# A mean over rows on one core: rewritten so that a partition owns 128 neighbouring rows, with loops, aligned buffers and one store

## The chip, the cores and the metric

The kernel runs on one core of a Trainium2 chip. The metric is the device time of one execution in microseconds (us); the median of the timed runs stands for a kernel. The core's engines are TensorE (PE, matrix products), VectorE (DVE), ScalarE (ACT), GpSimd (POOL) and SyncE (SP, which here only issues transfers). Each has its own program; they meet at semaphores. Sixteen DMA engines move data between the device memory (DRAM) and the on-chip memory (SBUF), which has 128 partitions; a tensor there has rows in partitions and columns along each of them. PSUM is a small memory that TensorE writes.

## The reference

```python
def setup_inputs():
    return {"x": np.random.randn(64, 256, 8192).astype(np.float32)}

def reference(x):
    return np.mean(x, axis=2)
```

So 64 x 256 = 16,384 rows of 8192 numbers (32 KiB) each become one number: 512 MiB are read, 64 KiB are written.

## The kernel before, in words

The input is seen as 16,384 rows. The kernel works in tiles of 256 rows (8 MiB): a partition of a tile gets two neighbouring rows, 64 KiB in one piece, into one of three buffers. `NB` = 63 tiles are done so; the last 256 rows are handled apart, as two tiles of 128 rows, `T0` and `T1`.

Which two rows a partition gets is set by the view `pairs`: partition 4m+w holds rows 64w+2m and 64w+2m+1 of the tile. So partitions 0, 4, 8 ... hold neighbouring pieces of 64 KiB, and partitions 0 to 3 hold pieces that lie 64 rows (2 MiB) apart.

The programs are unrolled: every tile has its own instructions on every engine.

- SP issues the load of tile g into buffer g mod 3 (line 106), after waiting until VectorE (line 104 or 105) and ScalarE have summed tile g-3. Then come `T0` in one load (line 109) and `T1` in seven loads of falling width (line 111): 4096, 2048, 1024, 512, 256, 128 and 128 columns, the last of them into the tensor `fin`. Then the stores: 63 KiB of results (line 115) and two rows of 128 results (line 118).
- VectorE sums the first row of each pair (line 129), ScalarE the second one, by a copy onto itself with a running total (line 153). In the last tile they share the one row of a partition by halves (lines 133, 139, 143 and 153); VectorE adds the partial sums (lines 136 and 147).
- The sums lie one per partition, and the result must lie along a row to be stored in long pieces: TensorE transposes them by an identity matrix that GpSimd builds (lines 87, 89, 184, 186, 189), and ScalarE copies them from PSUM, scaled by 1/8192 (line 157).

All loads and stores go through SP's one queue, in the order of issue. Semaphores count tiles done by VectorE (`dve_sem`) and ScalarE (`act_sem`), and landings for each buffer (`in_sems`).

The buffers are the first tensors of the kernel. The program's own placement puts them at byte 16,512 of each partition, 65,536 bytes apart; 16,512 is 64.5 times 256.

Of the kernel before, what the change touches and what calls it, by code (L numbers as in the profile page):

```python
# [4 lines left out]

F32 = mybir.dt.float32
ADD = mybir.AluOpType.add
X = mybir.AxisListType.X
COPY = mybir.ActivationFunctionType.Copy


def bass_global_avg_pool_1d_kernel(
    nc: bass.Bass,
    x: bass.AP,
    out: bass.AP,
):
    P = 128
    B, C, L = x.shape
    rows = B * C
    assert rows % (2 * P) == 0 and L % 64 == 0  # L20
    inv = 1.0 / float(L)

    NB = rows // (2 * P) - 1
    NBUF = 3
    assert NB >= NBUF

    flat = x.rearrange("b c l -> (b c) l")
    W = 4  # L30
    M = P // W
    pairs = flat.rearrange("(g w m j) l -> g m w (j l)", w=W, m=M, j=2)
    tiles = flat.rearrange("(t p) l -> t p l", p=P)
    T0, T1 = 2 * NB, 2 * NB + 1
    out_flat = out.rearrange("b c -> (b c)")
    out_pairs = out_flat.rearrange("(g q) -> g q", q=2 * P)
    out_tiles = out_flat.rearrange("(t p) -> t p", p=P)

    ch = [L // 2, L // 4, L // 8, L // 16, L // 32, L // 64, L // 64]
    assert sum(ch) == L
    NCH = len(ch)
    NS = 4
    offs = [sum(ch[:c]) for c in range(NCH)]
    NPART = 2 * NS + 2

    with ExitStack() as ctx:
        sb = lambda n, s: ctx.enter_context(nc.sbuf_tensor(n, s, F32))
        ps = lambda n, s: ctx.enter_context(nc.psum_tensor(n, s, F32))  # L50
        sem = lambda n: ctx.enter_context(nc.semaphore(n))
        bufs = [sb(f"buf{i}", [P, 2 * L]) for i in range(NBUF)]
        in_sems = [sem(f"in_sem{i}") for i in range(NBUF)]
        res = [sb(f"res{j}", [P, NB]) for j in range(2)]

        fin = sb("fin", [P, ch[-1] + NPART])
        half = sb("half", [P, 2])
        last = [sb(f"last{j}", [P, 1]) for j in range(2)]
        ident = sb("ident", [P, P])
        outsb = sb("outsb", [NB, 2 * P])  # L60
        row = [sb(f"row{j}", [1, P]) for j in range(2)]
        psum = [ps(f"psum{j}", [NB, P]) for j in range(2)]
        psum_row = [ps(f"psum_row{j}", [1, P]) for j in range(2)]
        dve_sem = sem("dve_sem")
        act_sem = sem("act_sem")
        ident_sem = sem("ident_sem")
        pe_sem = sem("pe_sem")
        cp_sem = sem("cp_sem")
        tile_sem = sem("tile_sem")
        out_sems = [sem(f"out_sem{i}") for i in range(3)]  # L70
        ch_sems = [sem(f"ch_sem{i}") for i in range(NCH)]
        pd_sem = sem("pd_sem")
        pa_sem = sem("pa_sem")

        tail = bufs[NB % NBUF]
        H = L // 2
        tile0 = tail[:, 0:L]
        part = lambda i: fin[:, ch[-1] + i : ch[-1] + i + 1]

        def chunk(c):  # L80
            if c == NCH - 1:
                return fin[:, 0 : ch[c]]
            return tail[:, L + offs[c] : L + offs[c] + ch[c]]


        eng = nc.gpsimd
        eng.memset(ident[:], 0.0).then_inc(ident_sem, 1)  # L87
        eng.wait_ge(ident_sem, 1)
        eng.affine_select(  # L89
            out=ident[:],  # L90
            in_=ident[:],
            compare_op=mybir.AluOpType.not_equal,
            fill=1.0,
            base=0,
            pattern=[[-1, P]],
            channel_multiplier=1,
        ).then_inc(ident_sem, 1)


        eng = nc.sync  # L100
        for g in range(NB):
            b = g % NBUF
            if g >= NBUF:
                eng.wait_ge(dve_sem, g - NBUF + 1)
                eng.wait_ge(act_sem, g - NBUF + 1)
            eng.dma_start(bufs[b][:], pairs[g]).then_inc(in_sems[b], 16)
        eng.wait_ge(dve_sem, NB - NBUF + 1)
        eng.wait_ge(act_sem, NB - NBUF + 1)
        eng.dma_start(tile0, tiles[T0]).then_inc(tile_sem, 16)  # L109
        for c in range(NCH):  # L110
            eng.dma_start(  # L111
                chunk(c), tiles[T1][:, offs[c] : offs[c] + ch[c]]
            ).then_inc(ch_sems[c], 16)
        eng.wait_ge(cp_sem, 2)
        eng.dma_start(out_pairs[0:NB, :], outsb[:, :]).then_inc(out_sems[0], 16)
        for j in range(2):
            eng.wait_ge(cp_sem, 3 + j)
            eng.dma_start(out_tiles[T0 + j : T0 + j + 1, :], row[j][:, :]).then_inc(
                out_sems[1 + j], 16
            )  # L120
        for s in out_sems:
            eng.wait_ge(s, 16)


        eng = nc.vector
        for g in range(NB):
            b = g % NBUF
            eng.wait_ge(in_sems[b], 16 * (g // NBUF + 1))
            eng.tensor_reduce(  # L129
                res[0][:, g : g + 1], bufs[b][:, 0:L], X, ADD  # L130
            ).then_inc(dve_sem, 1)
        eng.wait_ge(tile_sem, 16)
        eng.tensor_reduce(half[:, 0:1], tile0[:, 0:H], X, ADD).then_inc(dve_sem, 1)  # L133
        eng.wait_ge(act_sem, NB + 1)
        eng.wait_ge(dve_sem, NB + 1)
        eng.tensor_reduce(last[0][:], half[:], X, ADD).then_inc(dve_sem, 1)  # L136
        for c in range(NS):
            eng.wait_ge(ch_sems[c], 16)
            eng.tensor_reduce(part(c), chunk(c)[:, 0 : ch[c] // 2], X, ADD).then_inc(  # L139
                pd_sem, 1  # L140
            )
        eng.wait_ge(ch_sems[NCH - 2], 16)
        eng.tensor_reduce(part(NS), chunk(NCH - 2), X, ADD).then_inc(pd_sem, 1)  # L143
        eng.wait_ge(pa_sem, NS + 1)
        eng.wait_ge(ch_sems[NCH - 1], 16)
        eng.wait_ge(pd_sem, NS + 1)
        eng.tensor_reduce(last[1][:], fin[:], X, ADD).then_inc(dve_sem, 1)  # L147


        eng = nc.scalar  # L150

        def summed(ap, to, done):
            eng.activation(ap, ap, COPY, accum_out=to).then_inc(done, 1)  # L153

        def from_psum(n, dst, src):
            eng.wait_ge(pe_sem, n)
            eng.activation(dst, src, COPY, scale=inv).then_inc(cp_sem, 1)  # L157

        for g in range(NB):
            b = g % NBUF  # L160
            eng.wait_ge(in_sems[b], 16 * (g // NBUF + 1))
            summed(bufs[b][:, L : 2 * L], res[1][:, g : g + 1], act_sem)
        for j in range(2):
            from_psum(
                j + 1,
                outsb[:, :].rearrange("g (w m j) -> g j m w", w=W, m=M, j=2)[:, j],
                psum[j][:, :].rearrange("g (m w) -> g m w", m=M, w=W),
            )
        eng.wait_ge(tile_sem, 16)
        summed(tile0[:, H:L], half[:, 1:2], act_sem)  # L170
        for c in range(NS):
            eng.wait_ge(ch_sems[c], 16)
            summed(chunk(c)[:, ch[c] // 2 :], part(NS + 1 + c), pa_sem)
            if c == 0:
                from_psum(3, row[0][:, :], psum_row[0][:, :])
        eng.wait_ge(ch_sems[NS], 16)
        summed(chunk(NS), part(NPART - 1), pa_sem)
        from_psum(4, row[1][:, :], psum_row[1][:, :])


        eng = nc.tensor
        eng.wait_ge(ident_sem, 2)
        eng.wait_ge(dve_sem, NB)
        eng.transpose(psum[0][:, :], res[0][:, :], ident[:, :]).then_inc(pe_sem, 1)  # L184
        eng.wait_ge(act_sem, NB)
        eng.transpose(psum[1][:, :], res[1][:, :], ident[:, :]).then_inc(pe_sem, 1)  # L186
        for j in range(2):
            eng.wait_ge(dve_sem, NB + 2 + j)
            eng.transpose(psum_row[j][:, :], last[j][:, :], ident[:, :]).then_inc(  # L189
                pe_sem, 1  # L190
            )


# [26 lines left out]
```

## Time and profile before

| what | value |
|---|---|
| timed runs | 1247.22, 1247.23, 1247.58 us; median 1247.23 |
| span of the profiled execution, first to last instruction | 1246.1 us |
| around the span, to the median | 1.2 us |
| DMA | 536.97 MB, 10,303 packets, mean 431 GB/s |
| VectorE busy | 556.9 us (45%) |
| ScalarE busy | 459.2 us (37%) |
| TensorE and GpSimd busy | 1.4 and 0.7 us |

The profiled execution's own time is its span and what lies around it; the timed runs carry no profile of their own, so the 1.2 us is the span set against their median. A line of a group reads: line of the kernel, engine, operation, result<-source, shapes and number of instructions | busy time in us, mean ns of one | idle time of the engine ahead of them, and what ended it. The chain of waits follows the work back from the last instruction and is shown in order of time: start, length in us, and what it was; "issue" is time in which nothing recorded was waited for. The rows of digits show the busy share of 40 equal slices of the span in tenths.

### The profile page before, as it was taken

The page shows a single profiled execution, that of the slowest core. Times are in us where ns is not written, and L with a number is a line of the kernel's source. Part 1 is how long each engine was busy: PE and PEld are TensorE (multiplying, and loading weights), DVE is VectorE, ACT ScalarE, POOL GpSimd, SP SyncE. Part 2 cuts the span into 40 slices and gives each one's busy share as a digit, 9 for nine tenths or more (in the row PEclk, how much of TensorE's full clock was granted, in tenths as well). Part 3 has the DMA queues.
Part 4 walks back from the last instruction along what each step waited for, and adds up shares of the span by engine and source line. Part 5 has one row for each costly group of instructions (what it writes and reads, how often), then busy time and mean ns, then how long its engine had stood idle before and what let it go on. Part 6 is the DMA issues. An engine that isn't in the chain of part 4 may idle for free.

```text
span 1246.1 us, 383 instructions
## 1 busy us (share of the span) xinstructions
PE 1.4 (0%) x4; PEld 0.4 (0%) x4; DVE 556.9 (45%) x71; ACT 459.2 (37%) x143; POOL 0.7 (0%) x6
## 2 busy tenths in 40 slices
PE   0000000000000000000000000000000000000000
PEld 0000000000000000000000000000000000000000
DVE  2354453543534435345354453544535435344355
ACT  2243342442423424334243342433424324234245
POOL 0000000000000000000000000000000000000000
DMA  9999999999999999999999999999999999999998
GB/s 404 438 438 438 435 421 425 435 438 438 438 438 435 425 421 435 438 438 438 438 435 429 419 434 438 438 438 438 432 431 423 433 435 438 435 438 433 433 425 362
DMA packets 10303, 536.97 MB, mean 431 GB/s; under 512 B 1147, under 2 KB 1596, under 8 KB 1852
## 3 DMA queue, kind: packets, MB, share of 16 engines
q1 hardware_dynamic: 10300, 536.94, 99.7%
q14 instruction: 3, 0.02, 0.0%
HBM read 536.87 MB, written 0.07 MB: 431 GB/s over the span
## 4 chain that ended last, share of the span: by engine, by line
DMA 85%; DVE 15%; ACT 0%; SPq 0%; issue 0%; PE 0%
DMA buf<-in_x_dram 85%; DVE res L129 15%; ACT buf L153 0%; SPq L111 0%; PE psum_row L189 0%; SPq L109 0%; DVE last L147 0%; ACT row L157 0%
## 5 line engine op out<-in xcount | busy, mean ns | idle before, releaser
L129 DVE TENSOR_REDUCE res<-buf 128x1 f32<-128x8192 f32 x63 | 547.2, 8686 | 685.4 <-DMA buf<-in_x_dram 685.4
L153 ACT ACTIVATE buf<-buf 128x8192 f32<-128x8192 f32 (+3 forms) x69 | 450.9, 6535 | 782.0 <-DMA buf<-in_x_dram 782.0
L153 ACT ACTIVATION_READ_ACCUMULATOR buf<-buf 128x1 f32 x69 | 12.9, 187 | 0.0
L133 DVE TENSOR_REDUCE half<-buf 128x1 f32<-128x4096 f32 x1 | 4.4, 4420 | 1.0 <-DMA buf<-in_x_dram 1.0
L139 DVE TENSOR_REDUCE fin<-buf 128x1 f32<-128x2048 f32 (+3 forms) x4 | 4.5, 1153 | 0.5 <-DMA buf<-in_x_dram 0.4
L184 PE MATMUL psum<-ident,res 128*63 128x128 f32 x1 | 0.4, 444 | 1232.8 <-DVE res L129 1232.8
L153 ACT ACT_TABLE_LOAD x1 | 1.3, 1283 | 0.7 <-PEq L205 0.7
L157 ACT ACTIVATE outsb<-psum 63x128 f32<-63x128 f32 x2 | 0.6, 389 | 2.2 <-PE psum L184 2.2
L157 ACT ACTIVATE row<-psum_row 1x128 f32<-1x128 f32 x2 | 0.5, 258 | 0.8 <-PE psum_row L189 0.8
L189 PE MATMUL psum_row<-ident,last 128*1 128x128 f32 x2 | 0.7, 372 | 10.5 <-DVE last L147 5.5
L184 PEld LDWEIGHTS psum<-ident,res 128*63 128x63 f32 x1 | 0.2, 179 | 1232.7 <-issue 1232.7
L186 PE MATMUL psum<-ident,res 128*63 128x128 f32 x1 | 0.4, 421 | 0.0
L147 DVE TENSOR_REDUCE last<-fin 128x1 f32<-128x138 f32 x1 | 0.3, 297 | 0.1
L143 DVE TENSOR_REDUCE fin<-buf 128x1 f32<-128x128 f32 x1 | 0.3, 286 | 0.1
L89 POOL TENSOR_SCALAR_AFFINE_SELECT ident<-ident 128x128 f32<-128x128 f32 x1 | 0.3, 292 | 0.2 <-POOL ident L87 0.2
L186 PEld LDWEIGHTS psum<-ident,res 128*63 128x63 f32 x1 | 0.2, 230 | 0.0
L87 POOL MEMSET ident<- 128x128 f32 x1 | 0.2, 204 | 0.3 <-POOLq L205 0.3
L136 DVE TENSOR_REDUCE last<-half 128x1 f32<-128x2 f32 x1 | 0.2, 155 | 0.1
L189 PEld LDWEIGHTS psum_row<-ident,last 128*1 128x1 f32 x2 | 0.2, 79 | 11.2 <-DVE last L147 5.8
L205 POOL MEMSET const-bfloat16-1.0<- 128x1 bf16 x1 | 0.1, 101 | 0.0
L205 POOL MEMSET const-uint8-127<- 128x1 uint8 x1 | 0.1, 101 | 0.0
L205 POOL MEMSET const-float32-0.0<- 128x1 f32 x1 | 0.1, 98 | 0.2 <-issue 0.2
(1 smaller groups left out, 0.1 us busy)
## 6 DMA issues: line engine op xcount, KB each, us to landing
buf<-in_x_dram SPq DMA_DIRECT2D x1, 4096.0 KB, 39.7
buf<-in_x_dram SPq DMA_DIRECT2D x1, 2048.0 KB, 44.1
buf<-in_x_dram SPq DMA_DIRECT2D x1, 1024.0 KB, 46.1
buf<-in_x_dram SPq DMA_DIRECT2D x63, 49.3
buf<-in_x_dram SPq DMA_DIRECT2D x1, 512.0 KB, 47.0
buf<-in_x_dram SPq DMA_DIRECT2D x1, 256.0 KB, 47.1
buf<-in_x_dram SPq DMA_DIRECT2D x1, 128.0 KB, 47.0
buf<-in_x_dram SPq DMA_DIRECT2D x1, 64.0 KB, 46.7
```

Source lines behind the costliest of these rows:

```text
L89: eng.affine_select(out=ident[:], in_=ident[:], compare_op=mybir.AluOpType.not_equal, fill=1.0, base=0, pattern=[[-1, P]], channel_multipl ...
L129: eng.tensor_reduce(res[0][:, g : g + 1], bufs[b][:, 0:L], X, ADD).then_inc(dve_sem, 1)
L133: eng.tensor_reduce(half[:, 0:1], tile0[:, 0:H], X, ADD).then_inc(dve_sem, 1)
L139: eng.tensor_reduce(part(c), chunk(c)[:, 0 : ch[c] // 2], X, ADD).then_inc(pd_sem, 1)
L143: eng.tensor_reduce(part(NS), chunk(NCH - 2), X, ADD).then_inc(pd_sem, 1)
L147: eng.tensor_reduce(last[1][:], fin[:], X, ADD).then_inc(dve_sem, 1)
L153: eng.activation(ap, ap, COPY, accum_out=to).then_inc(done, 1)
L157: eng.activation(dst, src, COPY, scale=inv).then_inc(cp_sem, 1)
L184: eng.transpose(psum[0][:, :], res[0][:, :], ident[:, :]).then_inc(pe_sem, 1)
L186: eng.transpose(psum[1][:, :], res[1][:, :], ident[:, :]).then_inc(pe_sem, 1)
L189: eng.transpose(psum_row[j][:, :], last[j][:, :], ident[:, :]).then_inc(pe_sem, 1)
L205: nc = _bacc.Bacc("TRN2", target_bir_lowering=False, num_devices=1)
```

## The change

A partition now owns 128 neighbouring rows (4 MiB of the input): partition p has rows 128p to 128p+127. Tile i takes rows 2i and 2i+1 of every partition, again 64 KiB in one piece for each, and the pieces of a tile lie 4 MiB apart. The two last rows of each partition take the place of `T0` and `T1`; the last one comes in six loads (4096, 2048, 1024, 512, 256 and 256 columns) instead of seven.

SP, VectorE and ScalarE run loops over three tiles each (21 rounds) instead of unrolled programs; addresses of loads, results and waits are computed from the loop's counter. One semaphore per buffer (`free_sems`) is raised by both VectorE and ScalarE and replaces the two counts. ScalarE's table load stands inside its loop, ahead of the first sum.

The results of a partition are now neighbours in the output, so nothing is transposed: TensorE, PSUM and the identity are gone. ScalarE scales as it sums, into every second column of `outsb`; VectorE scales its 63 sums in one instruction, and adds and scales the partial sums of the last two rows with `total`. One store of 128 partitions with 512 bytes each stands at the end.

The small tensors are allocated ahead of the buffers, padded to multiples of 256 bytes; `pad0` and `pad1` hold nothing. The buffers begin at byte 24,576 of each partition, 96 times 256.

```diff
@@ -21,174 +22,145 @@
     inv = 1.0 / float(L)
+    R = rows // P
+    NBUF = 3
+    NLOOP = (R // 2 - 1) // NBUF
+    assert NLOOP * NBUF == R // 2 - 1 and NLOOP >= 2
...
-    W = 4
-    M = P // W
-    pairs = flat.rearrange("(g w m j) l -> g m w (j l)", w=W, m=M, j=2)
-    tiles = flat.rearrange("(t p) l -> t p l", p=P)
...
-    out_pairs = out_flat.rearrange("(g q) -> g q", q=2 * P)
...
+    own = x.rearrange("b c l -> (b c) l").rearrange("(p r) l -> p (r l)", p=P)
+    out_own = out.rearrange("b c -> (b c)").rearrange("(p r) -> p r", p=P)
-    ch = [L // 2, L // 4, L // 8, L // 16, L // 32, L // 64, L // 64]
+    ch = [L // 2, L // 4, L // 8, L // 16, L // 32, L // 32]
     assert sum(ch) == L
     NCH = len(ch)
-    NS = 4
+    NS = NCH - 2
     offs = [sum(ch[:c]) for c in range(NCH)]
-    NPART = 2 * NS + 2
+    NPART = 2 * NS + 1
     with ExitStack() as ctx:
         sb = lambda n, s: ctx.enter_context(nc.sbuf_tensor(n, s, F32))
...
         sem = lambda n: ctx.enter_context(nc.semaphore(n))
+        sb("pad0", [P, 32])
+        fin = sb("fin", [P, 320])
+        scaled = sb("scaled", [P, 320])
+        half = sb("half", [P, 64])
+        scaled_half = sb("scaled_half", [P, 64])
+        res = sb("res", [P, R])
+        outsb = sb("outsb", [P, R])
+        sb("pad1", [P, 960])
         bufs = [sb(f"buf{i}", [P, 2 * L]) for i in range(NBUF)]
         in_sems = [sem(f"in_sem{i}") for i in range(NBUF)]
-        res = [sb(f"res{j}", [P, NB]) for j in range(2)]
+        free_sems = [sem(f"free_sem{i}") for i in range(NBUF)]
+        row_sem = sem("row_sem")
+        ch_sems = [sem(f"ch_sem{i}") for i in range(NCH)]
+        act_sem = sem("act_sem")
+        dve_sem = sem("dve_sem")
+        out_sem = sem("out_sem")
...
-        psum_row = [ps(f"psum_row{j}", [1, P]) for j in range(2)]
...
+        tail = bufs[0]
         H = L // 2
...
         def chunk(c):
             if c == NCH - 1:
                 return fin[:, 0 : ch[c]]
             return tail[:, L + offs[c] : L + offs[c] + ch[c]]
...
+        part = lambda i: fin[:, ch[-1] + i : ch[-1] + i + 1]
         eng = nc.sync
-        for g in range(NB):
...
-            eng.dma_start(bufs[b][:], pairs[g]).then_inc(in_sems[b], 16)
...
-        eng.dma_start(tile0, tiles[T0]).then_inc(tile_sem, 16)
+        for b in range(NBUF):
+            eng.dma_start(bufs[b][:], own[:, 2 * b * L : 2 * (b + 1) * L]).then_inc(
+                in_sems[b], 16
+            )
+        with eng.Fori(1, NLOOP) as i:
+            for b in range(NBUF):
+                eng.wait_ge(free_sems[b], i * 2)
+                eng.dma_start(
+                    bufs[b][:], own[:, bass.ds((i * NBUF + b) * (2 * L), 2 * L)]
+                ).then_inc(in_sems[b], 16)
+        eng.wait_ge(free_sems[0], 2 * NLOOP)
+        eng.dma_start(tail[:, 0:L], own[:, (R - 2) * L : (R - 1) * L]).then_inc(
+            row_sem, 16
+        )
         for c in range(NCH):
-            eng.dma_start(
...
-        eng.dma_start(out_pairs[0:NB, :], outsb[:, :]).then_inc(out_sems[0], 16)
...
-            eng.dma_start(out_tiles[T0 + j : T0 + j + 1, :], row[j][:, :]).then_inc(
...
+            a = (R - 1) * L + offs[c]
+            eng.dma_start(chunk(c), own[:, a : a + ch[c]]).then_inc(ch_sems[c], 16)
+        D_SCALE, D_HALF, D_ROW = 1, 2, 3
+        D_PART = D_ROW + NS + 1
+        D_LAST = D_PART + 1
+        A_HALF = 1
+        A_PART = A_HALF + NS
+        eng.wait_ge(dve_sem, D_LAST)
+        eng.dma_start(out_own, outsb[:]).then_inc(out_sem, 16)
+        eng.wait_ge(out_sem, 16)
         eng = nc.vector
-        for g in range(NB):
...
-            eng.tensor_reduce(
...
+        with eng.Fori(0, NLOOP) as i:
+            for b in range(NBUF):
+                eng.wait_ge(in_sems[b], i * 16 + 16)
+                eng.tensor_reduce(
+                    res[:, bass.ds(i * NBUF + b, 1)], bufs[b][:, 0:L], X, ADD
+                ).then_inc(free_sems[b], 1)
+        def total(to, junk, ap, after):
+            eng.wait_ge(dve_sem, after)
+            eng.tensor_scalar(
+                junk, ap, inv, None, MULT, ADD, accum_out=to
             ).then_inc(dve_sem, 1)
...
-        eng.tensor_reduce(half[:, 0:1], tile0[:, 0:H], X, ADD).then_inc(dve_sem, 1)
...
-        eng.tensor_reduce(last[0][:], half[:], X, ADD).then_inc(dve_sem, 1)
...
+        for b in range(NBUF):
+            eng.wait_ge(free_sems[b], 2 * NLOOP)
+        n = R // 2 - 1
+        eng.tensor_scalar(
+            outsb[:, 0 : R - 2].rearrange("p (n j) -> p j n", j=2)[:, 0],
+            res[:, 0:n],
+            inv,
+            None,
+            MULT,
+        ).then_inc(dve_sem, 1)
+        eng.wait_ge(row_sem, 16)
+        eng.tensor_reduce(half[:, 0:1], tail[:, 0:H], X, ADD).then_inc(dve_sem, 1)
+        eng.wait_ge(act_sem, A_HALF)
+        total(outsb[:, R - 2 : R - 1], scaled_half[:, 0:2], half[:, 0:2], D_HALF)
+        for c in range(NS + 1):
             eng.wait_ge(ch_sems[c], 16)
-            eng.tensor_reduce(part(c), chunk(c)[:, 0 : ch[c] // 2], X, ADD).then_inc(
...
-        eng.tensor_reduce(part(NS), chunk(NCH - 2), X, ADD).then_inc(pd_sem, 1)
...
+            share = chunk(c)[:, 0 : ch[c] // 2] if c < NS else chunk(c)
+            eng.tensor_reduce(part(c), share, X, ADD).then_inc(dve_sem, 1)
+        eng.wait_ge(act_sem, A_PART)
         eng.wait_ge(ch_sems[NCH - 1], 16)
...
-        eng.tensor_reduce(last[1][:], fin[:], X, ADD).then_inc(dve_sem, 1)
+        w = ch[-1] + NPART
+        total(outsb[:, R - 1 : R], scaled[:, 0:w], fin[:, 0:w], D_PART)
         eng = nc.scalar
+        with eng.Fori(0, NLOOP) as i:
+            for b in range(NBUF):
+                eng.wait_ge(in_sems[b], i * 16 + 16)
+                ap = bufs[b][:, L : 2 * L]
+                eng.activation(
+                    ap,
+                    ap,
+                    COPY,
+                    scale=inv,
+                    accum_out=outsb[:, bass.ds((i * NBUF + b) * 2 + 1, 1)],
+                ).then_inc(free_sems[b], 1)
-        def summed(ap, to, done):
...
+        def summed(ap, to):
+            eng.activation(ap, ap, COPY, accum_out=to).then_inc(act_sem, 1)
-        def from_psum(n, dst, src):
...
-        for g in range(NB):
...
-            summed(bufs[b][:, L : 2 * L], res[1][:, g : g + 1], act_sem)
...
-        summed(tile0[:, H:L], half[:, 1:2], act_sem)
+        eng.wait_ge(row_sem, 16)
+        summed(tail[:, H:L], half[:, 1:2])
         for c in range(NS):
             eng.wait_ge(ch_sems[c], 16)
-            summed(chunk(c)[:, ch[c] // 2 :], part(NS + 1 + c), pa_sem)
...
-        summed(chunk(NS), part(NPART - 1), pa_sem)
...
-        eng.transpose(psum[0][:, :], res[0][:, :], ident[:, :]).then_inc(pe_sem, 1)
...
-        eng.transpose(psum[1][:, :], res[1][:, :], ident[:, :]).then_inc(pe_sem, 1)
...
-            eng.transpose(psum_row[j][:, :], last[j][:, :], ident[:, :]).then_inc(
...
+            summed(chunk(c)[:, ch[c] // 2 :], part(NS + 1 + c))
 # ---- launch: one core; inputs and outputs as the reference has them ----
```

## The prediction

> **What bounds the kernel now.** I read the page first, for who is busy. The DMA rows come first, then the two compute rows:
>
> ```profile
> DVE  2354453543534435345354453544535435344355
> ACT  2243342442423424334243342433424324234245
> DMA  9999999999999999999999999999999999999998
> ...
> q1 hardware_dynamic: 10300, 536.94, 99.7%
> ...
> L129 DVE TENSOR_REDUCE res<-buf 128x1 f32<-128x8192 f32 x63 | 547.2, 8686 | 685.4 <-DMA buf<-in_x_dram 685.4
> L153 ACT ACTIVATE buf<-buf 128x8192 f32<-128x8192 f32 (+3 forms) x69 | 450.9, 6535 | 782.0 <-DMA buf<-in_x_dram 782.0
> ```
>
> One queue keeps the 16 DMA engines busy for 99.7% of the span; VectorE and ScalarE are half idle, and all of that idle time before their big sums ends with a landing. The chain of waits, in order of time, gives the beat:
>
> ```profile
> 23.34 8.70 DVE res L129
> 32.04 0.02 issue
> 32.05 49.32 DMA buf<-in_x_dram
> 81.37 0.02 issue
> 81.40 8.70 DVE res L129
> ...
> 1242.31 0.02 issue
> 1242.33 1.54 ACT buf L153 x6
> 1243.87 0.03 issue
> 1243.90 0.31 DVE last L147
> 1244.21 0.04 issue
> 1244.26 0.39 PE psum_row L189
> 1244.64 0.02 issue
> 1244.66 0.27 ACT row L157
> ```
>
> From 23.34 to 81.40 three tiles of 8 MiB land: 58.06 us, 19.35 each, 433 GB/s. VectorE needs 8.7 of each 19.35. So 63 tiles make 1219 us of the 1246.1, and only two things can move the time: what one packet costs a DMA engine, and the pieces at both ends (the first tile lands at 23.3, some 4 us more than a beat; from the last landings to the end some 3.8 us).
>
> The trace also keeps one record per DMA packet. A big load is 128 packets of 65,536 bytes, eight on each engine, back to back. In the first tiles an engine starts one every 2414 ns; later every 2414 to 2429 ns, 2419 on average (19.35/8).
>
> **The change part by part.** The profiled execution spans 1246.06 us; the median of the timed runs is 1247.23, so 1.17 us lie around the span. I change the sum against the span and add the 1.17 back.
>
> *Buffers at multiples of 256 bytes.* Before, the buffers begin at byte 16,512 of a partition (128 past such a multiple), after at 24,576. The 512-byte packets of the last loads start 23.5 ns apart, the big ones 2414. The difference, 2390.5 ns over 65,024 bytes, is 36.8 ps a byte; 512 bytes are then 18.8 ns, and 4.7 ns of every packet, large or small, are not bytes. After, an engine has 63x8 + 7x8 = 560 packets. If the placement causes all of it, 2.63 us go; if none, 0. Against: the 4-byte semaphore packet, which has nothing to do with the buffers, also holds its engine some 6 ns. For: all loads, whatever their size, show the same extra, and all begin 128 bytes off. I take 2.63 and keep 0 for a rival. The Trainium skill's page "DMA: Bandwidth & Descriptors", section "How a descriptor splits into AXI transactions", says that a transfer starting off a 256-byte boundary pays for the bytes below its start, in beats of 32 bytes; four beats for 128 bytes would be the 4.7 ns, and the sum by it is the one I take.
>
> *What the packets lose later.* 19.353 less 8x2.414 and 0.006 is 0.035 us a tile, 2.2 us over 63. The trace doesn't show the cause; the pattern repeats from tile to tile, so other addresses may end it (-2.2), leave it (0) or worsen it (the rival on pitch). No row is nearer to either end of a gain; I take half, -1.1.
>
> *A partition owns 128 neighbouring rows.* A tile's 128 blocks of 64 KiB lay in four runs, neighbours 64 KiB apart; now each lies 4 MiB from the next. Sizes, counts and order of issue stay. The nearest row is the last tiles' loads, with rows 32 KiB apart: their 32,768-byte packets take 1213 to 1224 ns, the same time per byte. So a pitch changed by half cost nothing, and I take 0; but that row is far away, and the upper end stands among the rivals.
>
> *Loops.* Each engine's program becomes a loop of three tiles: registers, a branch, waits against register values. SP has issued three tiles ahead, so a late issue is covered by two queued tiles, 38.7 us. VectorE has 10.7 us idle per tile, ScalarE 12.2. ScalarE's table load now stands inside the loop: 21 times 1.28 us, one per three tiles, within that idle time. Were the cover gone, because a load took less than about 9 us a tile, these would count; it can't. Cost 0. The two semaphores per buffer become one that both engines raise: the same later one decides.
>
> *The last sums.* Before, ScalarE's six sums end at 1243.87, then VectorE, the transpose and ScalarE's copy run to 1244.93. After, ScalarE has one sum less (done near 1243.5), and VectorE runs on from 1242.33: 512 columns 0.69, 256 columns 0.42, the whole fifth piece of 256 another 0.42, so 1243.9, and then a scaling sum over 265 columns. Sums of 138 and 256 columns took 0.297 and 0.419; 265 are 0.43, and up to 0.62 if the running total has to be read out as ScalarE's does (0.187). The result is there at 1244.36 to 1244.55: 0.38 to 0.57 earlier, I take 0.45. TensorE's transposes, the copies from PSUM and GpSimd's identity go; all but the last ones lay beside loads and are worth 0. One load less (eight 4.7 ns packets' overhead and a semaphore) is 0.05.
>
> *One store.* Before, the last thing was one row of 512 bytes: 1244.93 to the end at 1246.06, 1.13 us, while the 63 KiB store lay hidden. Now all 64 KiB, 128 packets, go at the end, behind the last sum, with SP waiting for nothing else. Low end: as before plus eight packets on an engine, +0.2. High end: the first load, also 128 packets into an idle queue, was issued at 0.73; ten engines began between 2.17 and 2.30, the last one at 3.64, 2.9 after issue; with 0.2 and the 0.37 from the last packet to the end that is 3.48, +2.35. I go by the ten: 1.57+0.2+0.37, +1.0.
>
> Sum: -2.63 -1.1 -0.45 -0.05 +1.0 = -3.2. Span 1242.8, time 1244.0 us, 0.26% less. A measurement of this kernel tells about 0.2% (2.5 us) from no change.
>
> **The rivals.**
>
> 1. *The placement brings nothing.* Per-packet cost is the engine's own. For it: the semaphore packet. Against: the equal extra on all loads. Then +0 to -2.2, -0.5, +0.2 to +2.35: 1245.0 to 1249.1, most likely 1246.8, no change.
> 2. *The pitch slows the loads a little.* If every packet took what the slow ones take now, 2429 ns for 2419, 504 of them add 5 us, and without the 1.1: 1250. It decides once a packet lengthens by over 6.3 ns (3.2 us over 504). For it: packets differ by up to 15 ns today, so the loads do feel something.
> 3. *The pitch slows the loads greatly.* Sixteen blocks read at once, at addresses equal in their low 22 bits, could ask for the same part of the memory at the same time, every time, and nothing in the program would spread them again. The only slow packets of this trace are the first sixteen, all engines starting together: 2.42 to 3.64 us, median 3.30. At 3.30 throughout: 504x3.30 = 1663, the last two rows 19.4x1.365 = 27, some 9 at both ends: about 1700 us. Then the ends don't matter. For it: no load of this trace has a pitch above 64 KiB within a run, so none shows that it is harmless. Against: those first packets may be start-up alone, the second ones already take 2418, and the halved pitch changes nothing. The same page, section "Latency and other measured facts", reports copies within the memory at half the rate when rows lie 4 MiB apart and full rate with 4 KiB more, and guesses at aliasing. By its ratio, 103 to 214, this kernel would take some 2,550 us (an estimate from that page); no run here shows such a pitch.
>
> **How the numbers follow.** Forecast 0.37 (its own range 1242.0, all ends good, to 1244.7); rival 1 0.16, of it 0.02 slower by over 0.2%; rival 2 0.13; rival 3 0.34. Faster is the forecast, 0.37; within 0.2% the rest of rival 1, 0.14; slower 0.02+0.13+0.34 = 0.49. The forecast is the likeliest single case, though the slower ones together outweigh it. The range goes from 1242 to 1705: half of rival 3 (0.17) may lie above, 0.02 below.
>
> **What would show it.** Held rate: three tiles in 58.06 us or less in the chain, GB/s at 433 or above, VectorE's idle time before its sum still 10.6 us a tile. Placement: packets starting 2409 to 2410 ns apart, three tiles in 57.95. Store: some 2.1 us from its issue to the end; last sum at 0.43 to 0.62. Wrong: longer waits of VectorE and ScalarE for landings, GB/s below 430 in all slices alike (rivals 2 and 3), or a beat unchanged to the nanosecond (rival 1).

## The result, and the profile after

| kernel | timed runs, us | ratio to before (95% interval) |
|---|---|---|
| before | 1247.22 to 1247.58, median 1247.3 | 1 |
| changed | 1635.86, 1656.65, 1706.20, 1719.98; median 1681.43 | 1.3198 (1.3114 to 1.3283) |

The changed kernel is slower by about a third, and its own time varies by 5% from run to run; the ratio goes by its two faster runs (mean 1646.3 us), and the profile is of one of the two slower ones (span 1704.9 us), a difference on which nothing below rests.

The page of the changed kernel, cut to the lines that answer to those shown of before:

```profile
span 1704.9 us, 759 instructions
...
DVE  2242423233242424233242323424324324433344
...
DMA  8999999999999999999999999999999999999997
GB/s 271 309 304 295 308 315 308 301 295 317 301 309 303 300 298 312 320 306 311 304 320 323 303 315 303 323 323 321 318 329 331 335 331 329 354 360 369 360 383 181
...
q1 hardware_dynamic: 10224, 536.94, 98.5%
...
L109 DVE TENSOR_REDUCE res<-buf 128x8192 f32 x63 | 547.2, 8686 | 1128.9 <-DMA buf<-in_x_dram 1128.9
```

The DMA engines are as busy as before (98.5% against 99.7%) and move the same bytes, but at some 300 GB/s in place of 433, rising to 383 towards the end. VectorE's sums take the same 8686 ns each; its idle time ahead of them grew from 685 to 1129 us, 444 us, and all of it ends with a landing (the arrival of a load's data). The span grew by 459. So "busy" says nothing here about speed: a packet holds its engine longer.

The trace's packet records say the same (65,536-byte packets, 8064 of them; "by time" are means over the first, the eleventh and the last twentieth of them, in order of start):

| kernel | least, ns | median | mean | by time |
|---|---|---|---|---|
| before | 2415 | 2422 | 2423 | 2448 / 2421 / 2421 |
| changed | 2415 | 3334 | 3268 | 3395 / 3331 / 2685 |

504 packets on each engine by 3268 ns are 1647 us. The least packet is as short as before: some packets still pass at the old rate.

### The profile page after: what moved, and what is told of

Read it like the earlier page. It is cut to its first block, busy times and chain, and to the rows that moved or that the text cites. A ratio compares the mean times of both kernels' runs of the same rounds, so it can differ in the third digit from the quotient of the medians.

```text
span 1704.9 us, 759 instructions
## 1 busy us (share of the span) xinstructions
DVE 557.4 (33%) x74; ACT 483.7 (28%) x157; POOL 0.2 (0%) x4
## 3 DMA queue, kind: packets, MB, share of 16 engines
q1 hardware_dynamic: 10224, 536.94, 98.5%
## 4 chain that ended last, share of the span: by engine, by line
another core or an unknown queue 75%; DVE 23%; DMA 2%; issue 0%; DVEq 0%
DVE res L109 22%; DMA buf<-in_x_dram 2%; DVE fin L136 0%; DVE half L130 0%; DVEq L109 0%; DVEq L106 0%; DVE scaled L115 0%; DVE outsb L122 0%; DVE scaled_half L115 0%; DVEq L114 0%; DVEq L120 0%
## 5 line engine op out<-in xcount | busy, mean ns | idle before, releaser
L109 DVE TENSOR_REDUCE res<-buf 128x8192 f32 x63 | 547.2, 8686 | 1128.9 <-DMA buf<-in_x_dram 1128.9
L148 ACT ACTIVATE buf<-buf 128x8192 f32<-128x8192 f32 x63 | 442.9, 7030 | 783.9 <-DMA buf<-in_x_dram 783.7
L157 ACT ACTIVATE buf<-buf 128x4096 f32<-128x4096 f32 (+4 forms) x5 | 7.6, 1526 | 19.8 <-DMA buf<-in_x_dram 19.7
L148 ACT ACTIVATION_READ_ACCUMULATOR buf<-buf x63 | 11.7, 186 | 0.0
L136 DVE TENSOR_REDUCE fin<-buf 128x1 f32<-128x256 f32 (+3 forms) x5 | 5.0, 1006 | 7.2 <-DMA buf<-in_x_dram 7.2
L157 ACT ACTIVATION_READ_ACCUMULATOR buf<-buf 128x1 f32 x5 | 0.9, 186 | 0.0
```

The lines of the kernel that those rows point to most:

```text
L109: eng.tensor_reduce(res[:, bass.ds(i * NBUF + b, 1)], bufs[b][:, 0:L], X, ADD).then_inc(free_sems[b], 1)
L136: eng.tensor_reduce(part(c), share, X, ADD).then_inc(dve_sem, 1)
L148: eng.activation(ap, ap, COPY, scale=inv, accum_out=outsb[:, bass.ds((i * NBUF + b) * 2 + 1, 1)],).then_inc(free_sems[b], 1)
L157: eng.activation(ap, ap, COPY, accum_out=to).then_inc(act_sem, 1)
```

## The experiments

The theory after the result is that the loads are slowed by their places, 128 blocks whose addresses are equal in the low 22 bits. The rivals are that one of the other parts (loops, buffers' place, table load) slows them, or that the distance does, with sixteen places spread over the whole input read at once. Not all of these kernels compute the reference: some store results in other places, some sum overlapping rows, as the expectations say.

**The changed kernel with the old places of the loads (`near`).** The line in SP's loop stands for all loads; the first three and the last two rows are changed alike.

```diff
...
-                    bufs[b][:], own[:, bass.ds((i * NBUF + b) * (2 * L), 2 * L)]
+                    bufs[b][:], pairs[bass.ds(i * NBUF + b, 1)]
...
```

> The changed kernel with the loads' places of the kernel before (blocks 64 KiB apart in four runs), all else as changed; its results are stored in the changed kernel's order, so they stand in other places of the output. If the pitch of 4 MiB is what slows the loads: 1244 to 1248 us, 65,536-byte packets at 2414 to 2429 ns. If the loops, the buffers' new place or the other parts slow them: 1600 to 1720 us. It also measures what all the other parts are worth together: by my sum -3.2 us without the pitch (ratio 0.9974), by the rival in which the placement brings nothing between -2.3 and +1.9 us.

Measured 1244.33 us (1244.19 to 1244.52), ratio 0.9977 (0.9968 to 0.9986). One part of the change, the places, takes the kernel from 1244 to 1681 us; all the others together gain 2.9. The chain of waits of this kernel, in order of time:

```profile
32.21 48.98 DMA buf<-in_x_dram
...
81.31 8.70 DVE res L112
...
90.17 48.97 DMA buf<-in_x_dram
...
139.27 8.70 DVE res L112
```

Three tiles now come in 57.96 us (81.31 to 139.27), where before they took 58.06.

**The kernel before with the new places alone (`far_unrolled`).**

```diff
+    pairs = flat.rearrange("(p g j) l -> g p (j l)", p=P, j=2)
+    tiles = flat.rearrange("(p t) l -> t p l", p=P)
```

> The kernel before, unrolled, buffers at 16,512, with only the loads' places of the changed kernel (4 MiB apart); results in other places of the output. If the pitch is the cause: 1630 to 1720 us. If it is one of the other parts: 1247 us.

Measured 1677.1 us (1622.7 to 1731.5), packets of 3317 ns on average. The same edit from the other side: no loop, no padding, and the whole loss.

**A pitch of 126 rows (`pitch126`).** Distance stays, equal low bits go.

```diff
+    PITCH = R * L - 2 * L
+    own = bass.AP(tensor=own.tensor, offset=0, ap=[[PITCH, P], [1, R * L]])
```

> The changed kernel with a pitch of 126 rows (4 MiB less 64 KiB) in place of 128; the partitions' rows overlap, so some rows are summed twice and some not at all. If addresses equal in their low 22 bits collide: full rate, 1244 to 1250 us. If the distance alone does it (sixteen places spread over the whole input, whatever their low bits): 1630 to 1720 us as with 128.

Measured 1243.75 us (1243.65 to 1244.04), ratio 0.9973 (0.9962 to 0.9983); the median packet takes 2418 ns. Blocks 64 KiB less than 4 MiB apart, spread over nearly the whole input, load at full rate. The distance is out as the cause; what matters is the pitch itself, with 4 MiB exactly against 64 KiB less.

**The order reversed (`reversed`).** Every partition's tiles are read from the last to the first; the first three loads are changed like the line shown.

```diff
...
-                    bufs[b][:], own[:, bass.ds((i * NBUF + b) * (2 * L), 2 * L)]
+                    bufs[b][:], own[:, bass.ds((R - 4) * L - (i * NBUF + b) * (2 * L), 2 * L)]
```

> The changed kernel with the 63 tiles of every partition read from the last to the first; results in other places of the output. The packets got shorter towards the end of the changed kernel's run (mean 3.4 us in the first half, 2.7 in the last twentieth). If the address makes them shorter: short packets now at the start, long ones at the end. If time does (engines drifting apart): long at the start and short at the end as before. Total 1630 to 1720 us by both.

Measured 1680.7 and 1760.7 us, the second above the range expected. The row of GB/s over the span of this kernel:

```profile
GB/s 275 300 300 293 306 297 315 289 304 301 303 297 315 300 317 306 304 323 293 312 306 326 309 323 323 312 340 331 334 336 347 353 354 357 382 376 386 376 380 187
```

Slow at the start and faster at the end again (packets 3574 ns in the first twentieth, 2727 in the last). The recovery goes with time and not with the address.

**Other pitches (`pitch2m`, `pitch512k`, `minus4k`, `minus512`).** The same one line has other numbers for `PITCH`; the one of `pitch2m` is shown.

```diff
-    PITCH = R * L - 2 * L
+    PITCH = R * L - 64 * L
```

> The changed kernel with a pitch of 2 MiB in place of 4; partitions overlap, rows are summed twice or not at all. If only addresses equal in their low 22 bits collide, two places are left and the loads get a good part of the loss back: packets between 2.42 and 3.27 us, 1300 to 1500 us. If any power of two of this size collides fully: 1630 to 1720 us. If full rate returns: 1244 us.

> The same with a pitch of 512 KiB: addresses differ in three more bits than with 4 MiB. If these bits spread the blocks over the memory: full rate, 1244 us. If a large power of two is enough to collide: above 1500 us.

> A pitch of 4 MiB less 4 KiB; most rows are summed from parts of two rows. If what counts is where in a 4 MiB stretch the sixteen blocks begin, 128 blocks now spread over 508 KiB: full rate, 1244 us. If the shift has to be a whole block of 64 KiB, as in the pitch of 126 rows: 1630 to 1720 us.

> A pitch of 4 MiB less 512 bytes: the 128 blocks begin within 64 KiB of each other, modulo 4 MiB. If it is enough that engines do not read the same low address at the same moment: full rate, 1244 us. If blocks within one stretch of 64 KiB collide whatever their order: 1600 to 1720 us.

| pitch | time, us (median) | packets, ns: first twentieth / mean of all |
|---|---|---|
| 4 MiB (changed) | 1681.4 | 3395 / 3268 |
| 4 MiB - 512 bytes | 1272.3 (1270.1 to 1274.5) | 2630 / 2446 |
| 4 MiB - 4 KiB | 1244.3 (1244.0 to 1244.3) | 2456 / 2421 |
| 4 MiB - 64 KiB | 1243.8 | 2446 / 2420 |
| 2 MiB | 1265.7 (1265.1 to 1266.2) | 2875 / 2448 |
| 512 KiB | 1244.3 (1244.1 to 1244.5) | 2452 / 2420 |

512 KiB and 4 MiB less 4 KiB came as expected. The other two were missed: 2 MiB cost 21 us where I expected 50 to 250, and with 512 bytes less I had looked for all of the loss or none, and 28 us of 437 were left. The row of GB/s with 2 MiB shows why the loss is small:

```profile
GB/s 332 383 400 417 429 431 437 439 431 435 437 433 431 431 431 431 431 433 431 437 437 437 431 441 433 431 431 431 431 431 431 433 437 433 446 439 431 431 430 270
```

It begins slow, like the changed kernel, and is near full rate (429) in the fifth of forty slices. So the loads sort themselves out in time: in some 150 us with 2 MiB, and with 4 MiB not within 1700 us; with 512 KiB there is nothing to sort out (2452 ns in the first twentieth, 2453 in `near`). Where the pitch is below 4 MiB the partitions' rows overlap, and bytes are read more than once; for 512 KiB `blocks512k` below shows the same without overlap, for 2 MiB no run does.

**One load under way at a time (`far_one`, and `near_one` as its control).** If engines get out of each other's way by drifting apart, a start in common for each tile must undo it. `far_one` is the kernel before with loads 4 MiB apart, `near_one` with its own places; both get this wait:

```diff
+            if g:
+                eng.wait_ge(in_sems[(g - 1) % NBUF], 16 * ((g - 1) // NBUF + 1))
             eng.dma_start(bufs[b][:], pairs[g]).then_inc(in_sems[b], 16)
```

> The kernel before with the loads 4 MiB apart, and each load issued only after the one before it has landed, so that all sixteen engines begin every tile together; results in other places of the output. With three loads under way the packets fell from 3.4 us at the start to 2.9 at the end. If that is because the engines drift apart in their places: no fall here, packets of 3.3 us or more to the end, and some 3 us per tile between landing and next start, 1850 to 2000 us. If they fall for another reason, they fall here too, to 3.0 us or less.

> The kernel before with each load issued only after the one before it has landed, places of the loads unchanged. It is the control for the same wait with loads 4 MiB apart (2102 us, packets of 3.67 us on average). If the wait itself lengthens packets, because all engines begin together: packets well above 2.42 us here too. If it takes both, the common start and the equal addresses: 2.42 us but for the first packet of each engine and tile, and some 3.5 to 4 us per tile from landing to next data, 1450 to 1500 us.

Measured 2108.6 us (2103.5 to 2113.7) and 1448.2 us (1447.2 to 1449.2). The chain of waits of `far_one`:

```profile
0.74 34.67 DMA buf<-in_x_dram
...
35.42 33.29 DMA buf<-in_x_dram
...
68.73 33.69 DMA buf<-in_x_dram
...
102.51 33.92 DMA buf<-in_x_dram
```

and of `near_one`:

```profile
0.73 22.78 DMA buf<-in_x_dram
...
23.53 22.51 DMA buf<-in_x_dram
...
46.06 22.52 DMA buf<-in_x_dram
```

The wait costs `near_one` 3.2 us a tile: the first packet of each engine holds it for 3.25 us on average, all others for 2.42. In `far_one` the later packets are no shorter than the first: 3.53 us for the first sixteen of a tile, 3.69 for the rest. The wait alone does not lengthen the later packets; loads 4 MiB apart do, and with the wait by more than without it (3.67 us on average against 3.32 in `far_unrolled`). The fall over the run is smaller, but not gone: from the first to the last quarter 3740 to 3610 ns, where `far_unrolled` has 3467 to 3066. In time `far_one` came out above the 1850 to 2000 us expected, `near_one` just below its 1450 to 1500.

The trace also keeps sixteen landing signals for every load, which I take to be one per engine; the time from the first to the last of them says how far apart the engines are. In the changed kernel it grows from 0.85 us in the first tile to 21.5 in the last. With 2 MiB it grows from 1.8 to 5.6 us over the first eight tiles, while the packets (means of a tile) come down from 3050 to 2420 ns, and then it stays between 5.2 and 5.7. In `far_one` it stays between 0.8 and 1.6 us to the end. In `near`, at full rate, it is 0.4 to 0.5 us: engines close together are slow only with the far places. So the engines do drift apart where the loss shrinks, and a common start for each tile keeps them together; that the drift is what shortens the packets is argued from this.

**The buffers' place (`before_aligned`, `near_unaligned`).** The kernel before gets 128 unused bytes ahead of its buffers, which puts them on a multiple of 256:

```diff
+        sb("pad0", [P, 32])
         bufs = [sb(f"buf{i}", [P, 2 * L]) for i in range(NBUF)]
```

> The kernel before with one unused tensor of 128 bytes ahead of the buffers, so that they begin at byte 16,640 of a partition, a multiple of 256; nothing else. In the changed kernel with the old places of the loads the packets started 2414 to 2415 ns apart throughout, not 2419. If the buffers' place does that: one tile every 19.32 us in place of 19.36, and 1244.2 to 1244.8 us. If the loop, the smaller programs or the absent TensorE do it: 1247.2 us, unchanged.

The edit against `near`, which takes its buffers off that multiple:

```diff
-        sb("pad1", [P, 960])
+        sb("pad1", [P, 992])
```

> The changed kernel with the loads' places of the kernel before and the buffers 128 bytes later, at 24,704; results in other places of the output. If the buffers' place is what the 2.9 us came from: about 1247 us, packets up to 2429 ns again. If the loop or another part is: 1244.3 us.

Measured 1244.91 us (1244.77 to 1245.04), ratio 0.9981 (0.9972 to 0.9990), and 1246.47 (1246.36 to 1246.68), ratio 0.9994 (0.9985 to 1.0003). One unused tensor of 128 bytes is worth 2.35 us to the kernel before; taking the alignment from `near` costs it 2.14. The chain of waits of `before_aligned`:

```profile
23.50 8.70 DVE res L130
...
32.22 49.27 DMA buf<-in_x_dram
...
81.51 8.70 DVE res L130
...
139.42 8.70 DVE res L130
```

57.91 us from 81.51 to 139.42. The packets' least spacing is 2414 ns with either place; off the boundary they are spaced 2414 to 2429, 2419 on average, on it 2414 or 2415 nearly throughout. This kernel computes the reference and is faster than both kernels of this study.

**Pitches for the whole output (`blocks1m`, `blocks512k`).** The changed kernel with blocks of 32 or 16 neighbouring rows per partition, SP unrolled:

```diff
...
+    RB = 32
+    Q = R // RB
+    blocks = x.rearrange("b c l -> (b c) l").rearrange(
+        "(q p r) l -> q p (r l)", q=Q, p=P
+    )
...
+    out_own = out.rearrange("b c -> (b c)").rearrange("(q p r) -> p q r", q=Q, p=P)
...
```

> The changed kernel with 32 neighbouring rows per partition in each of four parts of the input, so that loads lie 1 MiB apart; SP's loop is unrolled, and the one store has 512 pieces of 128 bytes. With 512 KiB the loads ran at full rate and with 2 MiB nearly. If 1 MiB is at full rate: 1244.3 us and up to 1 us more for the store, 1244.3 to 1245.3. If it has part of the loss: 1246 to 1260 us.

> The changed kernel with 16 neighbouring rows per partition in each of eight parts of the input: loads 512 KiB apart, SP's loop unrolled, one store of 1024 pieces of 64 bytes. 1 MiB apart cost some 20 us, most of them in the first quarter. If 512 KiB is free of that, as it was with overlapping rows: 1244.3 us and 1 to 2 us for the store, 1245 to 1246.5, between the kernel before with aligned buffers (1244.9) and the kernel before (1247.3). If the store's small pieces cost more than that: above 1247.

Measured 1264.32 us (1260.63 to 1267.09), ratio 1.0144 (1.0128 to 1.0160), and 1245.25 (1244.86 to 1245.62), ratio 0.9984 (0.9975 to 0.9993). The 1 MiB was a miss: it came out above the 1246 to 1260 us that I gave for a part of the loss. Its packets take 2673 ns in the first twentieth, 2433 in the third, 2428 in the last, so it loses as much as 2 MiB. With 512 KiB the change does what its other parts can give, and its store of 1024 pieces lands 2.2 us after its issue, against 1.5 for 128 pieces in `near`.

## Why the prediction was wrong

The forecast was 1244.0 us, faster; it came out at 1681. The range reached 1705 only for the sake of the third rival, which held 0.34, and the rival is what happened. Its sign, GB/s below 430 in all slices, came, but not "alike": the slices rise from 271 to 383.

- **The step that failed: "A partition owns 128 neighbouring rows", cost taken as 0.** It was measured as 437 us by the medians (`near` to the changed kernel; 392 to 476 for its single runs) and, by itself, 430 (before to `far_unrolled`): a packet held its engine for 3268 ns on average in place of 2423. The row that I went by, loads 32 KiB apart, says nothing of 4 MiB: 64 KiB (`near`) and 512 KiB are free too, and of the pitches tried 1 MiB is the first with a loss. I wrote that the row was far away, and still gave it the forecast.
- **The third rival is what happened, but its price came near by luck.** The 1700 us went by the first sixteen packets of before (median 3.30 us). `near_one` has such first packets in every tile at the old places, 3.25 us on average, with 2.42 for all others: they are long from the common start alone, which the prediction itself gave as the argument against, and they price no pitch. The packets of the changed kernel have a median of 3.33 us, but fall over the run, and take 3.69 in `far_one`. What the rival said of equal addresses held (`near`, `pitch126`, `minus4k`): after a common start the packets stay long with the far places (3.69 us in `far_one`) and not with the near ones (2.42 in `near_one`). "Nothing in the program would spread them again" is wrong: the loads do recover, in some 150 us with 2 MiB, and slowly with 4 MiB.
- The page that the prediction named for this rival, the Trainium skill's "DMA: Bandwidth & Descriptors", section "Latency and other measured facts", has the direction right. Its loss for copies within the memory, 103 against 214 GB/s, is larger than the one of the loads here (315 against 431 GB/s over the spans), its step from 207 at 512 KiB to 164 at 2 MiB is much larger than the 1.7% here, and its shift of 4 KiB, taken the other way, restores the full rate here too.
- **Placement, -2.63, and what the packets lose later, -1.1.** Together -3.73; measured -2.35 in the kernel before and -2.14 in `near`. The size was near, the split wrong: the 4.7 ns that every packet carries stayed (spacing 2414 with either place), and what went was the later 35 ns a tile, for which I had named no cause. The Trainium skill's page "DMA: Bandwidth & Descriptors", section "How a descriptor splits into AXI transactions", charges beats for the bytes below an unaligned start; taken to hold for the destination in SBUF, as the prediction took it, the fixed part should have gone with the alignment. The runs do not show that.
- **Loops, 0: right.** `near` and `pitch126` run with loop, register waits and 21 table loads at one tile every 19.32 us.
- **The last sums, -0.45 and -0.05.** From the last full tile's landing to the result it was 21.00 us before (1223.93 to 1244.93) and 20.17 in `near` (1221.14 to 1241.31): -0.83 where -0.50 was expected.
- **One store, +1.0.** From the result to the end 1.13 before, 1.59 in `near`: +0.46; the high end of 2.35 was far off.
- **The sum without the pitch** was -3.2; `near` measured -2.9. At the landing of the last full tile `near` is 2.79 us ahead (1221.14 against 1223.93); the placement's 2.1 to 2.4 is most of that, and the rest is not assigned.
- **A slip in rival 1:** its terms at their best give 1244.7 and not 1245.0; nothing hangs on it.

## What to carry to other kernels

When a layout puts the pieces that DMA engines read at the same time a large power of two apart, price it by an experiment or choose another pitch; here 1, 2 and 4 MiB cost 1.5%, 1.7% and 35% (by the medians), while 512 KiB, or 4 MiB less 4 KiB, cost nothing. Such a loss hides in a DMA share of 98.5%: look at GB/s and at VectorE's idle time ahead of its sums. And where the nearest row is a factor of 128 away from the new value, it is no forecast, in either direction: the last loads gave no cost, and the slow common start gave a price that was near by luck.

## What was not expected of the hardware

- Loads that slow each other sort themselves out by running on: with 2 MiB from 332 to 429 GB/s within the first five slices of forty. With three loads under way at 4 MiB the packets fell from 3.4 to 2.7 us over 1600 us, with the tiles in either order. The landing signals of a load spread meanwhile, from 0.85 to 21.5 us with 4 MiB; with a common start for each tile they stay within 1.6 us, and the packets fall only from 3.77 to 3.52 us. What in the memory the engines share was not tried.
- A pitch of 512 bytes less took the loss from 437 to 28 us, one of 4 KiB less all of it.
- Buffers 128 bytes off a multiple of 256 cost 2.1 to 2.4 us of 1247 (0.2%), not as a fixed price per packet but as spacings that vary between 2414 and 2429 ns.
- The loss at 4 MiB differs from run to run by up to 109 us (`far_unrolled`), where every kernel at full rate repeats within 0.8 us.
